# Products of zeros ahead of the first load: fp32r of several widths and divisions of the array in place of bf16 ones between the sums, with six more VectorE operations

## The chip, the cores and the metric

The kernel runs on one core of one Trainium2 chip. The metric is the device time of one execution in microseconds (us); runs of one kernel are compared by their median.

## The reference

Two layers of a diffusion trunk, over 256 latent and 256 context tokens of 2048 channels, all in float32. For each layer:

```
shift, scale, gate = split(silu(c) @ w_mod[l] + b_mod[l])        # the same with c_ctx for the context
h    = rmsnorm(x, g_pre[l]) * (1 + scale) + shift
proj = h @ w_in[l]                                               # 2048 x 5120 columns, nine groups
y    = concat(gated position mixing, windowed attention, Fourier mixing), each times its silu gate
x    = x + gate * rmsnorm(y @ w_out[l], g_post[l])
```

The context runs through the same weights, gives keys and values to the latent attention, and is updated in the first layer only. The output is the latent stream.

## The kernel before

x and the context are held transposed: 128 channels on the partitions (16 such blocks, numbered k), 512 tokens in the free dimension (256 latent, 256 context). A product with a float32 weight is made of fp32r products: ScalarE rounds the weight to a high part (`whi`, L535), VectorE subtracts for the low part (`wlo`, L537), and TensorE multiplies high by high, low by high and high by low (`mm3`, L566). The weights come in pieces of 128 x 1024 through three `raw` buffers, four `whi` and four `wlo` buffers (`Stream`, L462).

**The head** (L1483 to L1556) is written out by hand for TensorE, VectorE, ScalarE and SP: they keep the order of the text. SP and ScalarE issue eight loads of x, 512 KB each (L1488). VectorE clears constants and small buffers. Then a loop of 16 steps squares two blocks of x a step, on ScalarE, or on VectorE in steps 3, 8 and 13 (`XSQ`, L407), and TensorE sums the squares over the channels with a weight of ones of 32 columns (L1510). Four blocks go to four groups of 32 columns of the array (`tile_position=(0, 32 * ...)`). The squares lie in `w2k`, a tag of seven buffers, one of which holds the first constants until after the loop. When all is summed, ScalarE copies the sums (L1515), TensorE, VectorE and GpSimd make 1/rms of them (L1527, L593) and spread it over partitions (L1539), TensorE makes the first block of shift and scale (`Mod`, L173, products at L202, loads at L188), and `make_h0` (L664) makes the first h. Then **layer 0** begins: for each block k the products of three groups of columns (`ps_av`, at L802; `ps_au`, at L802 and L567), and beside them the shift and scale of block k + 1 from its 2 MB of modulation weights.

In the head stand products of zeros: `warm(idle, n)` (L607) issues n bf16 products of 128 columns of weights by 512, from the cleared tile `wz` (its name in the trace is `join`) to a bank of PSUM that nobody reads. In the loop stand 6 before the first step and 3 before steps 4, 8 and 12 (L1506); 2, 1 and 3 more stand behind the loop (L1522, L1534, L1551).

A tile that is asked for again under its tag takes the buffers in turn, and the new writer waits until the last reader of the old contents is through.

Of the kernel before, what the change touches and what calls it, by code (L numbers as in the profile page):

```python
# [7 lines left out]
F32 = mybir.dt.float32  # L8
F32R = mybir.dt.float32r
BF16 = mybir.dt.bfloat16  # L10
AF = mybir.ActivationFunctionType
ALU = mybir.AluOpType

P = 128
# [52 lines left out]
def trunk_kernel(ctx: ExitStack, tc: tile.TileContext, xT, xhalf, cT, wss, wsl, wmod, win, wout0, wout1, const, vec, rows,  # L67
                 wmat, bs, sink, out):
    nc = tc.nc
    V, A, G, PE, DMA = nc.vector, nc.scalar, nc.gpsimd, nc.tensor, nc.sync  # L70
# [6 lines left out]
    def sb(shape, dt, tag, bufs=1):  # L77
        cnt[0] += 1
        return pool.tile(shape, dt, tag=tag, bufs=bufs, name=f"{tag}_{cnt[0]}")

    def w2k(shape, dt=F32):
        return sb(shape, dt, "w2k", W2K)

    def mm_ps(name="mm"):
        cnt[0] += 1
        return psum.tile([P, 512], F32, tag="mm", bufs=6, name=f"ps_{name}_{cnt[0]}")

    def ms_ps(name="ms"):
        cnt[0] += 1
        return psum.tile([P, 512], F32, tag="ms", bufs=2, name=f"ps_{name}_{cnt[0]}")  # L90
# [19 lines left out]
    zero8 = sb([P, 8], F32, "zero8")  # L110
# [30 lines left out]
    def cc(name):  # L141
        o, w = COFF[name]
        return cst[:, o - P:o - P + w]

    def vc(l, name):
        o, w = VOFF[name]
        return vecs[:, l, o:o + w]
# [304 lines left out]
    NHI, NLO, NRAW = 4, 4, 3  # L452
# [9 lines left out]
    class Stream:  # L462
# [95 lines left out]
        def next(self):  # L558
            self.fetch()
            pace()  # L560
            self.pos += 1
            return self.out[self.pos - 1]
# [30 lines left out]
    def rstd_cols(sums, n, dim):  # L593
        t = sb([P, 4], F32, "rs_a", 2)
        V.tensor_scalar(out=t[:, :n], in0=sums, scalar1=1.0 / dim, scalar2=EPS, op0=ALU.mult, op1=ALU.add)
        r = sb([P, 4], F32, "rs_b", 2)
        G.tensor_tensor(out=r[:, :n], in0=t[:, :n], in1=mhalf[:, :n], op=ALU.pow)  # L597
        return r
# [6 lines left out]
    wz = sb([P, T], BF16, "join", 2)  # L605

    def warm(ps, n):  # L607

        for _ in range(n):
            PE.matmul(ps, wz[:, 0:P], wz, start=True, stop=True)  # L610
# [49 lines left out]
    def scale_x(k, rb, s, n=1):  # L660
        x = xx[2 * (k // 4) + s][:, k % 4:k % 4 + n]
        V.tensor_tensor(out=x, in0=x, in1=rb[:, s * S:(s + 1) * S].unsqueeze(1).to_broadcast([P, n, S]), op=ALU.mult)

    def make_h0(k, between=(), rb=None):  # L664

        new_h(k)
        t = w2k([P, T])
        for a, b in ((0, P), (P, S), (S, T)) if k == 1 else ((0, S), (S, T)):
            s = a // S
            if s and rb is not None:  # L670
                scale_x(k, rb, 1)
            A.activation(hh[k][:, a:b], x_at(k, a, b), AF.Identity, scale=gs[0][:, k, s:s + 1],
                         bias=sh[0][:, k, s:s + 1])
        next(iter(between), None)
        for s in range(2):
            sl = slice(s * S, (s + 1) * S)
            V.tensor_scalar(out=t[:, sl], in0=x_at(k, sl.start, sl.stop), scalar1=gs[0][:, k, s:s + 1],
                            scalar2=sh[0][:, k, s:s + 1], op0=ALU.mult, op1=ALU.add)
        V.tensor_tensor(out=hl[k], in0=t, in1=hh[k].bitcast(F32), op=ALU.subtract)
# [592 lines left out]
    def out_proj():  # L1272
        acc = sb([P, T], F32, "acc")
        cross = sb([P, T], F32, "kt1")
        state["phase"] = "out0"
        groups = [OUT[i] // 4 for i in range(0, KT, 4)]
        for g in groups[:2]:
            load_x0(g)
        for i, j in enumerate(OUT[:KT - HELD]):
            ps = tunit(T)  # L1280
            o_evac(j, ps, new_yo(j), acc, [0, 1], i == 0, cross)
            if i in (4, 8):
                load_x0(groups[1 + i // 4])
        held = []
        W.stop = len(W.src) // 2
        state["phase"] = ""
        for j in OUT[KT - HELD:]:
            held.append([W.next(), W.next()])
            ps = hold_unit(held[-1], LAT)
            o_evac(j, ps, new_yo(j), acc, [0], False, cross)  # L1290
        later.add(boundary(acc, cross), YX[0])
        W.stop = 0
        for _ in range(EARLY):
            W.emit()
        for i, j in enumerate(OUT[KT - HELD:]):
            ps = hold_unit(held[i], CTX)
            if i < HELD - 1:
                with low(200):
                    o_evac(j, ps, yo[j], acc, [1], False)
        state["late"] = lambda: o_evac(j, ps, yo[j], acc, [1], False)  # L1300
        later.flush()
        return acc
# [177 lines left out]

    EN = mybir.EngineType
    first_stage = ExitStack()
    with tc.manual_schedule(engines={EN.PE}):  # L1483

        first_stage.enter_context(tc.manual_schedule(engines={EN.DVE, EN.Activation, EN.SP}))
        G.dma_start(ct, cT)
        for i in range(8):
            (A if i == 1 else DMA).dma_start(xx[2 * (i % 4) + i // 4], xhalf[i // 4, i % 4])  # L1488
        raw = w2k([P, NFIRST])
        DMA.dma_start(raw, const[:, 0:NFIRST])  # L1490
        DMA.dma_start(vecs, vec)
        V.memset(wz, 0.0)
        A.activation(sb([P, 4], F32, "es", 2), zero4, AF.Silu)
        sq, idle = mm_ps("rs2"), mm_ps("idle")
        for i in range(KT):
            h, j = i // 8, i % 8
            x = xx[2 * (j // 2) + h][:, j % 2 * 2:j % 2 * 2 + 2]
            q = w2k([P, 2, S])
            if i in XSQ:
                V.tensor_tensor(out=q, in0=x, in1=x, op=ALU.mult)  # L1500
            else:
                A.activation(q, x, AF.Square)
            if i == KT // 2:
                A.activation(cs, ct, AF.Silu)
                V.tensor_copy(cpad[:, 2:].rearrange("p (k c) -> p k c", c=32)[:, :, 0:2], cs)
            if i % 4 == 0:  # L1506
                warm(idle, 3 if i else 6)
            for a in range(2):
                k = 2 * j + a
                PE.matmul(sq[32 * (k % 4):32 * (k % 4) + 32, h * S:(h + 1) * S], ones[:, 0:32], q[:, a],  # L1510
                          start=k < 4, stop=k >= KT - 4, tile_position=(0, 32 * (k % 4)))
        A.copy(identr, raw[:, 0:P])
        A.copy(cst[:, 0:NFIRST - P], raw[:, P:])
        row = w2k([P, T])
        A.copy(row, sq)  # L1515
        m = Mod(0)
        m.load()
        G.tensor_scalar(out=b1, in0=vc(0, "bmod")[:, 16:32], scalar1=1.0, scalar2=None, op0=ALU.add)
        G.tensor_tensor(out=b1g, in0=b1, in1=vc(0, "gpre"), op=ALU.mult)
        W.load()  # L1520
        m.rounds(1)
        warm(idle, 2)  # L1522
        r0 = []
        for h, ps in enumerate((ms_ps("rs"), mm_ps("rs"))):
            for j in range(2):
                c = slice(h * S + j * P, h * S + (j + 1) * P)
                PE.matmul(ps[:, j:j + 1], row[:, c], cc("sel")[:, 0:1], start=True, stop=True)  # L1527
            r0.append(rstd_cols(ps[:, 0:2], 2, D))
            if h == 0:
                sums = ps  # L1530
        ps = sums
        V.tensor_scalar(out=msx, in0=ps[:, 0:2], scalar1=1.0 / D, scalar2=EPS, op0=ALU.mult, op1=ALU.add)
        m.rounds(2)
        warm(idle, 1)  # L1534
        rb = ms_ps("rb")

        def spread(s):
            for j in (2 * s, 2 * s + 1):
                PE.matmul(rb[:, j * P:(j + 1) * P], r0[s][:, j % 2:j % 2 + 1].to_broadcast([P, P]), ident,  # L1539
                          start=True, stop=True)  # L1540

        spread(0)
        m.rounds(1)
        m.turn()
        scale_x(0, rb, 0)
        m.cols()
        spread(1)
        rb0 = sb([P, T], F32, "acc")
        e = W.emitting(512)
        next(e)  # L1550
        warm(idle, 3)  # L1551
        make_h0(0, e, rb)
        A.copy(rb0, rb)
        for s in range(2):
            scale_x(1, rb0, s, 2)
        state["e0"] = e  # L1556
        layer(0)
        state["acc"] = out_proj()
        layer(1)
        finish()  # L1560
# [77 lines left out]
```

## Time and profile before

| | us |
|---|---|
| median of 2 runs (1119.59 to 1120.44) | 1120.01 |
| span of the profiled execution, first to last instruction | 1117.0 |
| TensorE busy | 1107.8 (99%) |
| VectorE busy | 926.9 (83%) |
| ScalarE busy | 550.6 (49%) |
| GpSimd busy | 33.4 (3%) |
| first product of layer 0 (start, in the span) | 21.88 |

The profiled execution's own time is not listed beside its span; the median of the runs is 3.0 us above the span, and is used in its place.

How to read the lines: in the timeline each has its start, its length, the engine (PE is TensorE, PEld its loads of weights, DVE VectorE, ACT ScalarE, POOL GpSimd, SP the queue that issues loads), the line of the kernel, the operation, what it writes and reads, its shape, and how many were merged; in brackets stands how long the engine was idle before it, and what released it. A matmul's length holds the way through the array: products that follow each other start closer together than they are long, so their cost is read from start to start. In the groups of instructions the number behind the bar is the busy time of all, then the mean of one in ns. In the stretches (windows) the columns are length, busy time of TensorE, of its weight loads, VectorE, ScalarE and GpSimd, then the granted TensorE clock, the busy share of the DMA engines and GB/s. In the view of waits: who waited for what, us in total, how often, the longest.

### The profile page before, as it was taken

How to read it: one execution, taken by the hardware profiler on the slowest of the kernel's cores; microseconds unless marked ns; L12 is line 12 of the kernel's file. 1: busy time of each engine (PE TensorE's matmuls, PEld its weight loads, DVE VectorE, ACT ScalarE, POOL GpSimd, SP SyncE). 2: the span in 40 equal slices, each digit the busy share in tenths (PEclk: the TensorE clock that was granted, in tenths of full speed). 3: DMA queues.
4: the chain of work that ended last, by engine and by line, in shares of the span. 5: the costliest groups of instructions: out<-in, count | busy, mean ns of one | idle time of the engine just before them, and what ended most of it. 6: DMA issues, size and time to landing. Idle time of an engine off the chain costs nothing. (4 is left out here: it accounts for less than half of the span.)

```text
span 1117.0 us, 17368 instructions
## 1 busy us (share of the span) xinstructions
PE 1107.8 (99%) x6453; PEld 927.4 (83%) x6453; DVE 926.9 (83%) x1616; ACT 550.6 (49%) x1049; POOL 33.4 (3%) x43
## 2 busy tenths in 40 slices
PE   8999999999999999999999999999999999999998
PEld 4777888888888888888888888988888888888886
DVE  3677599999988897988999989496988789878883
ACT  4454823322235666632532324256665379867551
POOL 1000000000000000000000000030500000000000
PEclk9999999999999999999999999999999999999999
DMA  9999665567655343455466665385956686456972
GB/s 375 412 411 404 231 202 166 195 210 227 201 188 176 100 156 117 152 194 189 155 206 203 208 209 185 96 216 190 227 170 203 212 285 196 160 182 196 302 263 75
DMA packets 75525, 235.89 MB, mean 211 GB/s; under 512 B 8480, under 2 KB 15024, under 8 KB 75440
## 3 DMA queue, kind: packets, MB, share of 16 engines
q1 hardware_dynamic: 71088, 230.31, 61.4%
q0 software_dynamic: 4064, 3.69, 2.2%
q8 instruction: 50, 0.82, 0.3%
q10 hardware_dynamic: 288, 0.79, 0.2%
q14 instruction: 35, 0.29, 0.1%
HBM read 232.65 MB, written 2.10 MB: 210 GB/s over the span
## 5 line engine op out<-in xcount | busy, mean ns | idle before, releaser
L535 ACT CAST whi<-raw 128x1024 fp32r<-128x1024 f32 (+1 forms) x210 | 216.3, 1033 | 309.8 <-PE ps_t L568 203.0
L567 PE MATMUL ps_t<-hh,whi 128*128 128x512 f32 (+1 forms) x752 | 290.6, 386 | 0.0
L568 PE MATMUL ps_t<-hl,whi 128*128 128x512 f32 (+1 forms) x752 | 289.5, 385 | 0.0
L569 PE MATMUL ps_t<-hh,wlo 128*128 128x512 f32 (+1 forms) x752 | 289.5, 385 | 0.0
L537 DVE TENSOR_TENSOR wlo<-raw,whi 128x1024 fp32r<-128x1024 f32 (+1 forms) x210 | 251.2, 1200 | 42.3 <-ACT whi L535 36.0
L310 DVE SCALAR_TENSOR_TENSOR macc<-mraw,cs,macc 128x512 f32<-128x512 f32 x360 | 251.4, 746 | 13.8 <-DMA mraw<-in_wmod_dram 13.7
L723 PE MATMUL ps_t<-hh,whi 128*128 128x512 f32 x512 | 184.4, 398 | 0.0
L569 PEld LDWEIGHTS ps_t<-hh,wlo 128*128 128x128 f32 x752 | 141.3, 188 | 28.6
L567 PEld LDWEIGHTS ps_t<-hh,whi 128*128 128x128 f32 x752 | 141.3, 188 | 26.7
L568 PEld LDWEIGHTS ps_t<-hl,whi 128*128 128x128 f32 x752 | 141.4, 188 | 26.3
L724 PE MATMUL ps_t<-hh,wlo 128*128 128x256 f32 x512 | 143.4, 280 | 0.0
L723 PEld LDWEIGHTS ps_t<-hh,whi 128*128 128x128 f32 x512 | 96.1, 188 | 21.0
L724 PEld LDWEIGHTS ps_t<-hh,wlo 128*128 128x128 f32 x512 | 96.7, 189 | 0.4
L567 PE MATMUL ps_y<-whi,hh 128*128 128x512 f32 x104 | 41.4, 398 | 0.0
L569 PE MATMUL ps_y<-whi,hh 128*128 128x512 f32 x104 | 40.7, 391 | 0.0
L568 PE MATMUL ps_y<-wlo,hh 128*128 128x512 f32 x104 | 40.5, 390 | 0.0
L584 ACT CAST w2k<-ps_tp 128x512 fp32r<-128x512 f32 x40 | 23.4, 585 | 21.2 <-PE ps_scc L568 13.6
L585 DVE TENSOR_TENSOR w2k<-ps_tp,w2k 128x512 fp32r<-128x512 f32 x40 | 27.4, 686 | 3.5 <-ACT w2k L584 2.3
L597 POOL TENSOR_TENSOR rs_b<-rs_a,mhalf 128x2 f32<-128x2 f32 (+1 forms) x7 | 6.3, 897 | 751.8 <-DVE mx L1413 582.8
L1147 ACT ACTIVATE w2k<-w2k,den 128x512 f32<-128x512 f32 (+1 forms) x48 | 28.2, 647 | 0.7 <-DVE den L1142 0.6
L802 PE MATMUL ps_av<-whi,hh 128*128 128x512 f32 x64 | 24.4, 396 | 0.1
L567 PE MATMUL ps_o<-w2k,vv 128*128 128x256 f32 x80 | 24.4, 305 | 0.0
(493 smaller groups left out, 1822.6 us busy)
## 6 DMA issues: line engine op xcount, KB each, us to landing
raw<-in_win_dram SPq DMA_DIRECT2D x158, 512.0 KB, 4.2
mraw<-in_wmod_dram SPq DMA_DIRECT2D x128, 512.0 KB, 4.5
raw<-in_wout_dram SPq DMA_DIRECT2D x60, 512.0 KB, 4.5
mraw<-in_wsl_dram SPq DMA_DIRECT2D x12, 512.0 KB, 7.3
yy<-in_xhalf_dram SPq DMA_DIRECT2D x7, 512.0 KB, 7.4
mg<-in_wsl_dram SPq DMA_DIRECT2D x7, 512.0 KB, 8.7
mgl<-in_wsl_dram SPq DMA_DIRECT2D x7, 512.0 KB, 9.2
yy<-in_xhalf_dram POOLq DMA_DIRECT2D x28, 128.0 KB, 7.5
```

The lines of the kernel that those rows point to most:

```text
L310: V.scalar_tensor_tensor(out=acc[:, s], in0=w[:, kk % 2], scalar=c, in1=acc[:, s], op0=ALU.mult, op1=ALU.add)
L535: A.copy(ph, rc)
L537: self.last = V.tensor_tensor(out=pl, in0=rc, in1=ph.bitcast(F32), op=ALU.subtract)
L567: PE.matmul(ps, st[0], mv[0], start=start, stop=False)
L568: PE.matmul(ps, st[0], mv[1], start=False, stop=False)
L569: PE.matmul(ps, st[1], mv[0], start=False, stop=stop)
L584: A.copy(hi, src)
L585: V.tensor_tensor(out=lo, in0=src, in1=hi.bitcast(F32), op=ALU.subtract)
L723: PE.matmul(ps, w[0], h, start=k == 0, stop=False)
L724: PE.matmul(ps[:, 0:S], w[1], h[:, 0:S], start=False, stop=k == KT - 1)
L802: PE.matmul(ps, st[a], mv[b], start=start and (a, b) == (0, 0), stop=stop and (a, b) == (1, 0))
L1147: A.activation(prob[i][:, b * w:(b + 1) * w], prob[i][:, b * w:(b + 1) * w], AF.Copy, scale=den[:, c:c + 1])
```

## The change

`trial` is called once, after the bank `idle` is allocated and before the loop; `warm` goes from the loop. The three `warm` calls behind the loop stay.

```diff
+    def trial(idle):
+        z = sb([P, 1024], F32R, "whi", NHI)
+        o = sb([P, 1024], F32, "wlo", NLO)
+        V.memset(z.bitcast(F32), 0.0)
+        V.memset(o, 0.0)
+        banks = [idle] + [mm_ps("idle2") for _ in range(3)]
+        big = z[:, 0:512]
+        def go(n, kind):
+            for i in range(n):
+                if kind == "whole":
+                    PE.matmul(idle, z[:, 0:P], big, start=True, stop=True)
+                elif kind[0] == "rows":
+                    w = kind[1]
+                    h = w * (i % (P // w))
+                    PE.matmul(banks[i % (P // w)], z[h:h + w, 0:P], z[h:h + w, 0:512], start=True, stop=True,
+                              tile_position=(h, 0))
+                elif kind[0] == "narrow":
+                    PE.matmul(idle[0:kind[1]], z[:, 0:kind[1]], big, start=True, stop=True)
+                elif kind[0] == "short":
+                    PE.matmul(idle[:, 0:kind[1]], z[:, 0:P], z[:, 0:kind[1]], start=True, stop=True)
+                elif kind[0] == "bf":
+                    PE.matmul(idle[0:kind[1]], wz[:, 0:kind[1]], wz, start=True, stop=True)
+        go(6, ("bf", P))
+        go(3, ("short", P))
+        go(3, ("short", 256))
+        go(3, ("short", 384))
+        go(5, "whole")
+        go(8, ("rows", 64))
+        go(8, ("rows", 32))
+        go(3, ("narrow", 96))
+        go(3, ("bf", 96))
+        r = sb([P, 1024], F32, "raw", NRAW)
+        V.memset(r, 1.0)
+        for n in (512, 1024):
+            V.scalar_tensor_tensor(out=o[:, 0:n], in0=r[:, 0:n], scalar=zero8[:, 0:1], in1=o[:, 0:n], op0=ALU.mult, op1=ALU.add)
+            V.tensor_scalar(out=o[:, 0:n], in0=r[:, 0:n], scalar1=zero8[:, 0:1], scalar2=None, op0=ALU.mult)
+            V.tensor_tensor(out=o[:, 0:n], in0=r[:, 0:n], in1=o[:, 0:n], op=ALU.subtract)
...
         sq, idle = mm_ps("rs2"), mm_ps("idle")
+        trial(idle)
         for i in range(KT):
...
-            if i % 4 == 0:
-                warm(idle, 3 if i else 6)
             for a in range(2):
```

The trial takes one buffer each of `whi`, `wlo` and `raw` and three banks of PSUM. The pieces of weights that follow take the next buffers in turn; the third load of raw (L508) now takes the buffer that VectorE's six operations read.

TensorE's order in the loop, before, from the last of the first six products of zeros (`ps_idle`) to the second group of them; `ps_rs` are the sums, `w2k` the squares of steps 0 to 4, two blocks a row:

```order
L610 MATMUL ps_idle_112<-join_91 128x512
L1510 MATMUL ps_rs_27_111<-w2k_113,ones_72 32x256 x2
L1510 MATMUL ps_rs_27_111<-w2k_123,ones_72 32x256 x2
L1510 MATMUL ps_rs_27_111<-w2k_127,ones_72 32x256 x2
L1510 MATMUL ps_rs_27_111<-w2k_131,ones_72 32x256 x2
L610 LDWEIGHTS join_91
L610 MATMUL ps_idle_112<-join_91 128x512
```

The same place now: the last of the six bf16 products, then what stands between it and the sums (of the 16 products over 64 and 32 rows the first and the last two; `ps_idle_31` to `ps_idle_33` are the added banks), and the first sums:

```order
L1508 MATMUL ps_idle_112<-join_91 128x512
L1506 MATMUL ps_idle_112<-whi_113 128x128 x3
L1506 MATMUL ps_idle_112<-whi_113 128x256 x3
L1506 MATMUL ps_idle_112<-whi_113 128x384 x3
L1497 MATMUL ps_idle_112<-whi_113 128x512 x5
L1501 MATMUL ps_idle_112<-whi_113 128x512
...
L1501 MATMUL ps_idle_32_118<-whi_113 128x512
L1501 MATMUL ps_idle_33_119<-whi_113 128x512
L1504 MATMUL ps_idle_112<-whi_113 96x512 x3
...
L1552 MATMUL ps_rs_27_111<-w2k_170,ones_72 32x256 x2
L1552 MATMUL ps_rs_27_111<-w2k_174,ones_72 32x256 x2
```

All products of zeros of the loop stand ahead of the first sum now, 42 where 15 stood, and the 16 pairs of sums follow each other with nothing between them.

VectorE's order around its first square (`w2k`, from x in `yy`), before:

```order
L1492 MEMSET join_91 128x256
L120 MEMSET red_81 128x1 x2
L1500 TENSOR_TENSOR w2k_131<-yy_3_63 128x512
L1500 TENSOR_TENSOR w2k_154<-yy_2_62 128x512
L1505 COPY kt_16_79<-cs_78 128x16x2
```

And now:

```order
L120 MEMSET red_81 128x1 x2
L1488 MEMSET whi_113 128x1024
L1489 MEMSET wlo_114 128x1024
L1520 MEMSET raw_162 128x1024
L1522 SCALAR_TENSOR_TENSOR wlo_114<-raw_162,zero_14_76,wlo_114 128x512
L1523 TENSOR_SCALAR wlo_114<-raw_162,zero_14_76 128x512
L1524 TENSOR_TENSOR wlo_114<-raw_162,wlo_114 128x512
L1522 SCALAR_TENSOR_TENSOR wlo_114<-raw_162,zero_14_76,wlo_114 128x1024
L1523 TENSOR_SCALAR wlo_114<-raw_162,zero_14_76 128x1024
L1524 TENSOR_TENSOR wlo_114<-raw_162,wlo_114 128x1024
L1544 TENSOR_TENSOR w2k_182<-yy_3_63 128x512
```

The first square on VectorE, that of step 3, stands behind nine more operations; each of the last five of them reads or overwrites what the one before it wrote. ScalarE's and SP's orders are unchanged.

## The prediction

> **What bounds the kernel now.** The page first: its span and the share of TensorE; then the stretches of time (windows), to see whether the first stage is paced by TensorE or by the loads.
>
> ```profile
> span 1117.0 us, 17368 instructions
> PE 1107.8 (99%) x6453; PEld 927.4 (83%) x6453; DVE 926.9 (83%) x1616; ACT 550.6 (49%) x1049; POOL 33.4 (3%) x43
> 22.00:50.00 28.00, 27.97 (x339) 20.96 (x340) 16.61 (x38) 11.34 (x23) 0.00 (x0) 1.00 1.03 413
> 80.00:110.00 30.00, 30.00 (x365) 23.70 (x366) 23.59 (x46) 14.63 (x29) 0.00 (x0) 1.00 1.04 407
> ```
>
> TensorE is busy 99% of the span, and from 22 us on its busy column equals the length of the stretch. The DMA column (1.03, 1.04) is full there too, so both run level. Which of them sets the pace is read from the waits of the first 120 us:
>
> ```profile
> PEld ps_mod L202 <- DMA mraw<-in_wsl_dram: 0.3, 1, 0.3
> SPq L188 <- DMA mraw<-in_wsl_dram: 9.6, 12, 1.0
> ACT whi L535 <- DMA raw<-in_win_dram: 15.8, 5, 4.7
> ```
>
> TensorE waits for a load once, for 0.3 us; ScalarE's 15.8 us for raw weights are waits ahead of need (SP's row, from its own queue's waits, is for later). So TensorE is the pace, and what starts it later ends the kernel later. Where it starts is decided in the first 22 us, the only stretch that the change touches. The timeline:
>
> ```profile
> 2.03 2.74 PE L610 MATMUL ps_idle<-join 128*128 128x512 bf16 x6 [2.03 <-DVE red L120]
> 3.28 0.15 PEld L610 LDWEIGHTS <-join 128*128 128x128 bf16 x1 [0.28 <-issue]
> 3.71 0.15 PEld L610 LDWEIGHTS <-join 128*128 128x128 bf16 x1 [0.28 <-issue]
> 5.42 2.72 ACT L1502 ACTIVATE w2k<-yy 128x512 f32<-128x512 f32 x5 [2.76 <-DMA yy<-in_xhalf_dram]
> 5.63 0.69 DVE L1500 TENSOR_TENSOR w2k<-yy 128x512 f32<-128x512 f32 x1 [3.64 <-DMA yy<-in_xhalf_dram]
> 6.10 1.68 PE L1510 MATMUL ps_rs<-w2k,ones 128*32 128x256 f32 x16 [1.33 <-ACT w2k L1502]
> 7.71 0.82 PE L610 MATMUL ps_idle<-join 128*128 128x512 bf16 x3
> 9.41 0.21 ACT L1504 ACTIVATE cs<-ct 128x32 f32<-128x32 f32 x1
> 13.54 1.15 ACT L1502 ACTIVATE w2k<-yy 128x512 f32<-128x512 f32 x2 [0.73 <-DMA yy<-in_xhalf_dram]
> 14.22 1.15 PE L1510 MATMUL ps_rs<-w2k,ones 128*32 128x256 f32 x8 [0.17 <-ACT w2k L1502]
> 15.47 0.59 ACT L1515 COPY w2k<-ps_rs 128x512 f32<-128x512 f32 x1 [0.47 <-PE ps_rs L1510]
> 20.71 0.62 ACT L535 CAST whi<-raw 128x512 fp32r<-128x512 f32 x1 [4.65 <-DMA raw<-in_win_dram]
> 21.88 0.30 PEld L802 LDWEIGHTS ps_av<-whi,hh 128*128 128x128 f32 x2 [0.56 <-ACT hh L672]
> ```
>
> The sums of squares (L1510) follow the landing of x: the last two squares begin at 13.54, after a wait for x, end at 14.69, and the last sum ends at 14.22 + 1.15 = 15.37. From there a chain (copy, rstd, its spreading, the first modulation, hh) leads to the first product of layer 0 at 21.88. The fifteen products of zeros at L610 in this loop lie in TensorE's waits.
>
> **The change part by part.** Removed: those 15 bf16 products. They give back nothing by themselves, since the sums wait for x, whose last part lands at about 13.5 us. Added ahead of the sums in TensorE's order: 42 products; ahead of the square of step 3 in VectorE's: three memsets and six operations. The question is when TensorE is through with the 42 (call it T0), since no sum can start before.
>
> *Speed of TensorE.* The six bf16 products start 3.71 - 3.28 = 0.43 us apart; the three at 7.71 take 0.82 with a tail, about 0.22 each. The clock doubled in between. The view of the cores says when:
>
> ```profile
> core 0: 1117.0 us, clock 0.999
> ```
>
> A mean of 0.999 (0.9985 to 0.9995) is 0.6 to 1.7 us lost, so 1.1 to 3.4 us at half speed; counted from 2.03, with 3.71 still slow, it ended between 3.7 and 5.4. I take 4.9. fp32r at full speed, from later stretches:
>
> ```profile
> 700.20 0.39 PE L569 MATMUL ps_t<-hh,wlo 128*128 128x512 f32 x1
> 702.92 0.39 PE L569 MATMUL ps_t<-hh,wlo 128*128 128x512 f32 x1
> 163.02 0.28 PE L568 MATMUL ps_f<-mg,w2k 128*128 128x256 f32 x1
> 163.14 0.28 PE L569 MATMUL ps_f<-mg,w2k 128*128 128x256 f32 x1
> 162.80 0.19 PEld L567 LDWEIGHTS ps_f<-mg,w2k 128*128 128x128 f32 x1
> 162.91 0.19 PEld L568 LDWEIGHTS ps_f<-mg,w2k 128*128 128x128 f32 x1
> 46.56 1.08 PE L202 MATMUL ps_mod<-mraw,kt 128*32 128x128 f32 x32
> L202 PE MATMUL ps_mod<-mraw,kt 128*32 128x128 f32 x192 | 6.7, 276 | 0.0
> 46.56 0.81 PEld L202 LDWEIGHTS ps_mod<-mraw,kt 128*32 128x32 f32 x32 [0.35 <-issue]
> 48.45 0.30 PEld L802 LDWEIGHTS ps_av<-whi,hl 128*128 128x128 f32 x2 [0.20 <-issue]
> ```
>
> Twelve products of 512 columns from 700.20 to 702.92: 0.227 each. 256 columns: 0.12. Weights follow each other at 0.11, so 128 columns cost 0.11 (at half speed twice that), and 384, between 256 and 512, 0.17. The 32 products over column groups show that tiles side by side overlap: (1.08 - 0.28) / 32 = 0.03 each, where one alone would pass at 0.11. To and from such a division of the array the load of weights stands 0.35 and 0.20 us, about 0.2 of it unhidden.
>
> T0 with tiles overlapping: six bf16 end at 2.03 + 6 x 0.425 = 4.58; 3 of 128, the first two slow, 0.45, to 5.03; 3 of 256, 0.36, to 5.39; 3 of 384, 0.53, to 5.92; 5 of 512, 1.14, to 7.06; eight over 64 rows as four pairs, 0.2 + 0.92, to 8.18; eight over 32 rows as two fours, 0.2 + 0.46, to 8.84; three of 96 columns, 0.2 + 0.68, to 9.72; three bf16 of 96, 0.66, to 10.38; back to column groups 0.1: **T0 = 10.5**. No trace shows row groups. The two bounds are full overlap (10.5) and none, 4 + 6 more turns of 0.227, **12.8**. I take overlap, since the column groups, the nearest row, do overlap. If the clock doubles at 3.7, T0 falls by 0.5, at 5.4 it rises by 0.3. The Trainium skill ("TensorE: Matmul & The Clock Gate", Part 3 on packing) gives four row tiles of 512 columns 3.07 times the rate of one; by that the eight over 32 rows would take 0.6, as here with the switch; of two tiles it gives no figure, and no run here shows it.
>
> *VectorE.* The rows:
>
> ```profile
> 0.82 0.17 DVE L106 MEMSET ones<- 128x128 f32 x1 [0.82 <-PEq L1626]
> 1.07 0.49 DVE L116 MEMSET kt<- 128x514 f32 x1
> 1.92 0.07 DVE L120 MEMSET red<- 128x1 f32 x2
> L310 DVE SCALAR_TENSOR_TENSOR macc<-mraw,cs,macc 128x512 f32<-128x512 f32 x360 | 251.4, 746 | 13.8 <-DMA mraw<-in_wmod_dram 13.7
> L308 DVE TENSOR_SCALAR macc<-mraw,cs 128x512 f32<-128x512 f32 x24 | 10.7, 482 | 2.7 <-DMA mraw<-in_wmod_dram 2.6
> 25.90 0.33 SPq L508 DMA_DIRECT2D raw<-in_win_dram  x1
> L662 DVE TENSOR_TENSOR yy<-yy,acc 128x1024 f32<-128x1024 f32 x6 | 7.1, 1217 | 0.0
> ```
>
> Memset grows by (0.49 - 0.17) / 386 = 0.83 ns an element: 0.92 for 1024, three of them from 1.99 to 4.75; z is there at 2.9, before TensorE wants it at 4.6. Then 0.75 + 0.48 + 0.69 for 512 elements and, for 1024, 1.28 (bounds 0.75 and twice that), 0.75 (0.48 to 0.96), 1.22, with 0.05 for each dependence: 10.2. The square of step 3 (0.69, as at 5.63) ends at 10.9 in place of 6.3. TensorE needs it as the fourth sum, at about T0 + 0.5 = 11.0: it just hides behind T0; were TensorE free earlier, this would be the bound. The load of raw that now waits for VectorE is issued at 25.9, long after.
>
> *After T0.* The squares live in w2k, seven buffers, of which the constants hold one. So steps 0 to 5 are squared before T0, and step 6 waits until the first sum has freed its buffer: T0 + 0.7 (a square's end to its sum's end is 15.37 - 14.69 = 0.68 in the trace). From there ScalarE has eight squares at (2.72 - 0.61) / 4 = 0.53 apart and SiLU of c, 0.22: the last begins 7 x 0.53 + 0.22 = 3.93 later and lasts 0.61; its sum ends 0.68 after. In all T0 + 0.7 + 3.93 + 0.61 + 0.68 = T0 + 5.92, against 15.37: **delay = T0 - 9.45**. With 10.5 it is 1.05 us; with 12.8, 3.3 us. The lower end is 0: before T0 = 9.45 the landing of x decides as now.
>
> *What follows.* ScalarE's copy at 15.47, and by it the chain to 21.88, move by the delay. The weights (cast at 20.71) land when they did and are no longer close. After 22 us TensorE has no wait for a load to give the delay back from. The sum: 1117.0 + 1.05 = 1118.05 of span. The runs' median lies 3.0 above the profiled span (no time of the profiled execution itself is listed), so **1121.0 us**.
>
> **The rivals.**
>
> (a) *Row tiles do not overlap.* For it: no product over 64 or 32 rows stands in the trace, and weights of fp32 are loaded with each product. Against: column groups do overlap. 1120.0 + 3.3 = **1123.3**.
>
> (b) *Loads set the pace: not slower.* In 22 to 110 us the DMA is as full as TensorE. If the steps there really went at the loads' pace, a start 1 us later would only let the loads run ahead, and the end would stay. Place: the modulation weights at L202. It decides wherever their landing, not the end of the product before, releases TensorE. For it: 413 GB/s throughout, and SP waits for landings of earlier loads before it issues the next (9.6 us in the one row shown). Against: that single wait of 0.3 us. The whole 1.05 would be won back: **1120.0**.
>
> (c) *The clock falls back.* Between T0 and the first product of layer 0 TensorE now has only sums over 32 columns and short chain work, where three warm groups (7.71 and two later) stood before. If this counts as idle, TensorE runs at half speed from about 15 us until the dense work has filled some microseconds. Price from rows: 22 to about 25.4 at half speed loses 1.7, the chain's products from 15 to 22 about 1 more; with the delay of 1.05, 1120.0 + 3.75 = **1123.8**. For it: the three groups are gone. Against: by the rows at 6.10 and 14.22 TensorE is busy through most of the time of the sums themselves. The Trainium skill ("TensorE: Matmul & The Clock Gate", Part 1) has the clock halved after an idle window of 3.4 us; by that rule (c) needs the sums to count as idle, which no row here shows.
>
> **How the numbers follow.** Forecast 0.5, (a) 0.2, (b) 0.15, (c) 0.12; 0.03 for what I have not thought of. Time 1121.0. The range goes down to 1119.7, which holds (b) with half of the 0.9 us between the two runs, and up to 1123.8, which holds (a) and half of (c). All the cases lie within 4 us, 0.4%, while 2% (22.4 us), about what a measurement of this kernel can tell from no change, is far off: same 0.97, slower 0.02, faster 0.01.
>
> **What would show it.** In the profile after: six bf16 products 0.43 apart from 2.03; five of 512 columns 0.23 apart; the pairs over 64 rows starting together, and the fours; the first sum between 10 and 11, step 3's square from VectorE ending at about 10.9; the last sum ending near 16.4, ScalarE's copy at 16.5, the first product ps_av at 22.9; from there the same rows 1 us later to the end. Tiles at 0.23 us each mean (a); an unchanged time of the last ps_mod products near 117 us despite a later start means (b); products of ps_av 0.43 apart after 22 us mean (c). A first sum at 14 us or later, or a first stage that lengthens by more than the delay, would make the prediction wrong.

## The result and the profile after

The changed kernel takes 1133.95 us (median of 2 runs, 1133.09 to 1134.82) against 1120.01 us before: a ratio of 1.0124, with a 95% interval of 1.0095 to 1.0154. That is 13.9 us more, within 2%, slower by much more than the runs scatter, and above the forecast's range. The profiled execution took 1134.82 us; its page begins:

```profile
span 1133.0 us, 17429 instructions
PE 1124.0 (99%) x6477; PEld 934.6 (82%) x6480; DVE 935.8 (83%) x1625; ACT 550.8 (49%) x1049; POOL 33.8 (3%) x43
```

The span grew by 16.0 us (1133.0 against 1117.0), and TensorE's busy time by 16.2. (A run's time lies 1.8 us above its span: 1134.82 against 1133.0. So the profiled execution before took about 1118.8 us, less than either of the two runs behind the median of 1120.01, which is why the spans differ by more than the medians.) TensorE got no new wait to speak of: it is busy longer. The first question is how much of that lies in the head, where the change is. The timeline of the changed kernel, in the order of the prediction's steps (start, length, engine, line):

```profile
3.71 0.15 PEld L1508 LDWEIGHTS <-join 128*128 128x128 bf16 x1 [0.28 <-issue]
4.21 2.80 PE L1506 MATMUL ps_idle<-whi 128*128 128x128 f32 x9
6.81 1.42 PE L1497 MATMUL ps_idle<-whi 128*128 128x512 f32 x5
8.16 1.86 PE L1501 MATMUL ps_idle<-whi 64*128 64x512 f32 x16
9.95 0.94 PE L1504 MATMUL ps_idle<-whi 128*96 128x512 f32 x3
10.54 0.68 DVE L1544 TENSOR_TENSOR w2k<-yy 128x512 f32<-128x512 f32 x1
11.46 5.58 PE L1552 MATMUL ps_rs<-w2k,ones 128*32 128x256 f32 x62
16.87 0.39 PE L1552 MATMUL ps_rs<-w2k,ones 128*32 128x256 f32 x2
17.36 0.58 ACT L1557 COPY w2k<-ps_rs 128x512 f32<-128x512 f32 x1 [0.47 <-PE ps_rs L1552]
23.56 0.30 PEld L802 LDWEIGHTS ps_av<-whi,hh 128*128 128x128 f32 x2 [0.42 <-ACT hh L672]
```

The first sum starts at 11.46, and the first product of layer 0 at 23.56 in place of 21.88: 1.68 us later. So the head explains 1.7 of 16 us. Where do the rest arise? The groups of instructions give the first and the last start of each group (behind the three durations in ns), and the same group can be looked up in both kernels. Before:

```profile
L1029 PE MATMUL ps_mix<-ws,w2k x48: 270/275/348, 142.7 to 786.9; 128*128 128x128 f32 x48
L1225 PE MATMUL ps_v<-whi,hh x48: 389/398/403, 308.6 to 892.8; 128*128 128x512 f32 x48
L723 PE MATMUL ps_au<-hh,whi x32: 387/392/398, 730.4 to 762.0; 128*128 128x512 f32 x32
L1317 PE MATMUL ps_x<-identr,yy x32: 270/272/273, 1020.1 to 1053.4; 128*128 128x128 f32 x32
```

And after:

```profile
L1029 PE MATMUL ps_mix<-ws,w2k x48: 270/275/347, 145.6 to 800.3; 128*128 128x128 f32 x48
L1225 PE MATMUL ps_v<-whi,hh x48: 387/396/398, 314.7 to 907.1; 128*128 128x512 f32 x48
L723 PE MATMUL ps_au<-hh,whi x32: 392/394/396, 743.6 to 775.4; 128*128 128x512 f32 x32
L1317 PE MATMUL ps_x<-identr,yy x32: 270/272/273, 1034.8 to 1068.5; 128*128 128x128 f32 x32
```

The lag is 2.9 us at 142.7, 6.1 at 308.6, 13.2 at 730.4, 14.7 at 1020.1, and 16.0 at the end. It grows steadily through layer 0, hundreds of microseconds behind the last changed instruction, and only by another 2.8 us in layer 1. The stretches of time say what a growing lag without waits is. Before (length, then busy time and count of TensorE, of its weight loads, VectorE, ScalarE and GpSimd, then clock, DMA share and GB/s):

```profile
160.00:710.00 550.00, 550.00 (x2678) 461.89 (x2677) 495.15 (x801) 226.31 (x420) 0.00 (x0) 1.00 0.56 180
520.00:660.00 140.00, 140.00 (x620) 115.95 (x619) 128.88 (x188) 50.58 (x81) 0.00 (x0) 1.00 0.61 198
800.00:840.00 40.00, 40.00 (x241) 35.30 (x240) 36.34 (x76) 28.21 (x59) 1.75 (x1) 1.00 0.62 191
```

And after (the first and the last stretch moved by the lag):

```profile
163.00:723.00 560.00, 560.00 (x2677) 463.04 (x2676) 496.31 (x801) 226.42 (x419) 0.00 (x0) 1.00 0.56 177
520.00:660.00 140.00, 140.00 (x604) 113.58 (x603) 130.99 (x190) 49.32 (x77) 0.00 (x0) 1.00 0.61 196
814.00:854.00 40.00, 40.00 (x243) 35.65 (x243) 36.25 (x77) 28.58 (x62) 1.75 (x1) 1.00 0.62 185
```

The same 2677 products take 560 us where they took 550, at the same granted clock (1.00), with TensorE busy without a gap in both. Each product is slower: in 140 us of the products of 512 columns (L567 to L569), 604 pass where 620 did. By their start times they follow each other at 226.7 ns before and at 232.4 after (means over 520 to 660 us). In layer 1's stretch of alternating widths (800 to 840) nothing is lost. **One number carries the case: 5.7 ns per product, for products that the change doesn't touch.** The row of 520 to 660 us is the test in what follows, called the pace row: x620 is the old pace, x604 the slow one.

### The profile page after: what moved, and what is told of

It is laid out like the page before. It is cut to its first block, busy times and chain, and to the rows that moved or that the text cites. A ratio compares the mean times of both kernels' runs of the same rounds, so it can differ in the third digit from the quotient of the medians.

```text
span 1133.0 us, 17429 instructions
## 1 busy us (share of the span) xinstructions
PE 1124.0 (99%) x6477; PEld 934.6 (82%) x6480; DVE 935.8 (83%) x1625; ACT 550.8 (49%) x1049; POOL 33.8 (3%) x43
## 5 line engine op out<-in xcount | busy, mean ns | idle before, releaser
L567 PE MATMUL ps_t<-hh,whi 128*128 128x512 f32 (+1 forms) x752 | 294.0, 391 | 0.0
L569 PE MATMUL ps_t<-hh,wlo 128*128 128x512 f32 (+1 forms) x752 | 293.1, 390 | 0.0
L568 PE MATMUL ps_t<-hl,whi 128*128 128x512 f32 (+1 forms) x752 | 293.1, 390 | 0.0
L310 DVE SCALAR_TENSOR_TENSOR macc<-mraw,cs,macc 128x512 f32<-128x512 f32 x360 | 251.0, 743 | 11.5 <-DMA mraw<-in_wmod_dram 11.2
L569 PEld LDWEIGHTS ps_t<-hh,wlo 128*128 128x128 f32 x752 | 141.6, 188 | 31.7
L567 PEld LDWEIGHTS ps_t<-hh,whi 128*128 128x128 f32 x752 | 141.7, 188 | 29.6
L567 PE MATMUL ps_y<-whi,hh 128*128 128x512 f32 x104 | 41.7, 401 | 0.0
L569 PE MATMUL ps_y<-whi,hh 128*128 128x512 f32 x104 | 41.1, 395 | 0.0
L567 PE MATMUL ps_o<-w2k,vv 128*128 128x256 f32 x80 | 24.6, 307 | 0.0
```

The costliest lines, as they stand in the source:

```text
L310: V.scalar_tensor_tensor(out=acc[:, s], in0=w[:, kk % 2], scalar=c, in1=acc[:, s], op0=ALU.mult, op1=ALU.add)
L567: PE.matmul(ps, st[0], mv[0], start=start, stop=False)
L568: PE.matmul(ps, st[0], mv[1], start=False, stop=False)
L569: PE.matmul(ps, st[1], mv[0], start=False, stop=stop)
```

## The experiments

**Is it the chip, or the state in which TensorE's stream starts?** What could outlive the head? A way of streaming in which TensorE settles early (when its clock doubles while products run, or by the added kinds of products), or something that stays in place, such as where the tiles lie. Four kernels ran beside the kernel before (1119.70 us). `again` is the changed kernel, unaltered.

> The changed kernel once more, unaltered. What is to be explained: from the first product of layer 0 on, products of 512 columns in fp32r start 232.4 ns apart where they started 226.7 apart before, to the end of the kernel; the clock doubled at 7.0 us, while TensorE was streaming products of zeros, and at 4.9 us before, while it was idle. Theory 1 (the pace is set at the moment at which the clock doubles, by whether TensorE is streaming then): about 1134 us in every run in which the doubling falls into the stream, which here is nearly always. Theory 2 (the kinds of products set the pace): 1134 us in every run. Theory 3 (chance at each start): runs at both 1121 and 1134 us.

It took 1133.12 us (1.0121, 1.0106 to 1.0136), with x604 in the pace row: not the chip. `gap` lets TensorE stand idle ahead of the fp32r products. It moves VectorE's filling of `raw` and the first of the six operations ahead of the clearing of `z`; nothing is added:

```diff
-        V.memset(z.bitcast(F32), 0.0)
         V.memset(o, 0.0)
+        r = sb([P, 1024], F32, "raw", NRAW)
+        V.memset(r, 1.0)
+        V.scalar_tensor_tensor(out=o[:, 0:512], in0=r[:, 0:512], scalar=zero8[:, 0:1], in1=o[:, 0:512], op0=ALU.mult, op1=ALU.add)
+        V.memset(z.bitcast(F32), 0.0)
...
-        r = sb([P, 1024], F32, "raw", NRAW)
-        V.memset(r, 1.0)
...
```

> The same 42 products and VectorE operations, but z is cleared only after the clearing of r and the first VectorE operation, so that TensorE is idle from about 4.6 to 6.9 us, and all products of z come after that. Theory 1 (streaming at the doubling sets the pace): where the clock doubles in that gap, 226.7 ns per product of 512 columns in layer 0 and about 1121.5 us; where it doubles in the stream behind it, 232 ns and 1135 us. Theory 2 (kinds of products: all are there): 232 ns and 1134 us whatever the moment. A variant of theory 2, that the first fp32r products at half speed do it: 226.7 ns if the clock has doubled before 6.9 us.

1136.26 us (1.0144, 1.0127 to 1.0161), x604: the head is later still, the pace is as slow. By the trace's record of the clock it doubled at 10.5 us, in the stream behind the idle time, so this run does not tell the theories apart. `twelve` is the kernel before with twice the bf16 products ahead of the first sum, so that the clock doubles within an unbroken stream:

```diff
-                warm(idle, 3 if i else 6)
+                warm(idle, 3 if i else 12)
```

> The kernel before, with twelve bf16 products of zeros ahead of the first sum in place of six, so that TensorE streams from 2.0 to about 6.5 us without a pause, and no product of a new kind. Theory 1: the clock doubles in the stream, 232 ns per product of 512 columns, about 1134 us. Theory 2: no new kind, 226.7 ns and 1120 us.

1119.47 us (1.0000, 0.9990 to 1.0009). The pace is the old one, so the state of the stream at the doubling isn't the cause. The pace row of `twelve`:

```profile
520.00:660.00 140.00, 140.00 (x620) 115.91 (x619) 131.19 (x191) 50.50 (x81) 0.00 (x0) 1.00 0.61 201
```

`dve_only` has the change's tiles and VectorE operations, the old `warm` in the loop, and none of the new products:

```diff
-        go(6, ("bf", P))
...
-        go(3, ("bf", 96))
...
+            if i % 4 == 0:
+                warm(idle, 3 if i else 6)
```

> The kernel before with the new tiles (whi, wlo, raw, three banks) and all of the new VectorE operations, but without the new products; the bf16 products stand between the sums as before. Theories 1 and 2: 226.7 ns per product of 512 columns; the square of step 3 comes at 11 us in place of 6.3, so about 0.5 to 1 us later, 1121 us. A rival, that the buffers and banks, which are taken in another turn, make each product slower: 232 ns and 1134 us.

1135.29 us (1.0138, 1.0122 to 1.0153), although not one of the added products runs. Its pace row:

```profile
520.00:660.00 140.00, 140.00 (x604) 113.49 (x603) 132.39 (x193) 49.35 (x77) 0.00 (x0) 1.00 0.61 197
```

So the kinds of products fall too. What `dve_only` shares with the change are VectorE's operations and three tiles, asked for earlier than before.

**Where the tiles lie.** A tag gets its place in memory when it is first asked for. The trial asks for `whi`, `wlo` and `raw` ahead of all others of the head, and so moves them. The addresses in the built programs (bytes in a partition):

| | before | after |
|---|---|---|
| `whi`, first buffer | 105600 (128 modulo 256) | 74752 (0) |
| `wlo`, first buffer | 121984 (128) | 91136 (0) |
| `hh0` (all `hh` and `hl` alike modulo 256) | 138368 (128) | 138368 (128) |
| `hh0` - `whi`, modulo 256 | 0 | 128 |

TensorE reads `whi` or `wlo` and `hh` or `hl` in every one of the slowed products, one as weights, the other as the moving operand. Either the place of `whi` itself matters (theory A), or its distance to `hh` (theory R). Four kernels beside the kernel before (1119.54 us) set them against each other; the first three add no instruction to it, only small tiles that are there anyway are asked for earlier. `pair_shift` moves both by 128 bytes:

```diff
+        for tag in ("mx", "nm"):
+            sb([P, 4], F32, tag, 2)
         G.dma_start(ct, cT)
```

> The kernel before, in which 128 bytes of late small tiles (mx, nm) get their place ahead of the first loads. So the weights whi and wlo and the h tiles all lie 128 bytes further on: whi and hh start at 256 modulo 512 instead of 128, and their distance is as before. No work is added. Theory A (the absolute address of the weights sets the pace of an fp32r product: 128 modulo 256 is fast, 0 is slow): 232 ns per product of 512 columns, 1134 us. Theory R (the distance of weights and moving operand sets it): 226.7 ns, 1120 us.

`h_shift128` puts the same 128 bytes between `wlo` and `hh0`, so that `whi` stays and only the distance becomes 128:

```diff
         rb0 = sb([P, T], F32, "acc")
         e = W.emitting(512)
         next(e)
+        for tag in ("mx", "nm"):
+            sb([P, 4], F32, tag, 2)
```

> The kernel before, in which the same 128 bytes get their place between wlo and hh0: the weights stay at 128 modulo 512, hh and hl move to 256, so that the distance is 128, as in the changed kernel. No work is added. Theory R: 232 ns per product of 512 columns, 1134 us. Theory A of the weights: 226.7 ns, 1120 us. Theory A of the moving operand (128 fast, 0 modulo 256 slow): 1134 us, but then the changed kernel, whose hh lie where they lay before, is not explained.

`h_shift256` puts 256 bytes there (`mx`, `nm`, `den`, `skb`, `nskb`).

> As the one before with 256 bytes between (mx, nm, den, skb, nskb): weights at 128 modulo 512, hh and hl at 384. Theory R modulo 256: fast, 1120 us. Theory R modulo 512 or more: slow, 1134 us. Theory A: fast, 1120 us, by the weights' address as by the moving operand's modulo 256.

`after_aligned` is the whole change, with 128 bytes ahead of `whi`, so that the distance is 0 again:

```diff
+        for tag in ("rs_a", "rs_b"):
+            sb([P, 4], F32, tag, 2)
         G.dma_start(ct, cT)
```

> The changed kernel with all of its work, in which 128 bytes of small tiles (rs_a, rs_b) get their place ahead of the first new tile: whi and wlo lie at 128 modulo 512, as in the kernel before, and hh stay at 128, so the distance is 0 modulo 512 again. Theories A and R: 226.7 ns per product of 512 columns; what is left is the later start, 1.7 us: about 1121.7 us. If the new order of the tiles does it in another way (distances of several KB, the turn of buffers or banks): 232 ns and 1134 us.

The pace rows of `pair_shift`, `h_shift128`, `h_shift256` and `after_aligned`:

```profile
520.00:660.00 140.00, 140.00 (x619) 115.93 (x618) 129.92 (x189) 51.01 (x82) 0.00 (x0) 1.00 0.62 199
```

```profile
520.00:660.00 140.00, 140.00 (x604) 113.53 (x603) 129.41 (x188) 49.90 (x78) 0.00 (x0) 1.00 0.62 195
```

```profile
520.00:660.00 140.00, 140.00 (x620) 115.95 (x619) 128.96 (x188) 50.88 (x82) 0.00 (x0) 1.00 0.61 198
```

```profile
520.00:660.00 140.00, 140.00 (x619) 115.96 (x618) 131.38 (x192) 51.85 (x82) 0.00 (x0) 1.00 0.62 202
```

`pair_shift` took 1118.67 us (0.9995, 0.9986 to 1.0004): theory A falls. `h_shift128`, with no work added at all, took 1131.87 (1.0112, 1.0095 to 1.0129): 12.3 us for 128 bytes. `h_shift256` took 1119.36 (0.9997, 0.9988 to 1.0006): it is the distance modulo 256. `after_aligned` took 1120.56 (1.0012, 1.0003 to 1.0021): with the distance mended, the change's own work costs 1.0 us (0.3 to 2.4). It keeps the changed turn of the buffers and the three added banks, so these are not the cause.

**How the pace goes with the distance.** Four more kernels, beside the kernel before (1119.64 us), put other sizes at the same place as `h_shift128`: `skb` (32 bytes), `skb` and `nskb` (64), or `mx`, `nm` and `den` (192).

> The kernel before with 32 bytes (skb) between wlo and hh0, so that hh minus whi is 32 modulo 256. What is asked is how finely the distance counts. If 256 bytes are eight banks of 32 and a conflict arises only half a turn away: 226.7 ns per product of 512 columns, 1119.5 us. If any distance other than 0 modulo 256 costs: 232 ns, 1132 us. If the cost rises with the distance up to 128: about 228 ns, 1123 us.

> The same with 64 bytes (skb, nskb): distance 64 modulo 256. Half a turn only: 226.7 ns, 1119.5 us. Anything but 0: 232 ns, 1132 us. Rising with the distance: about 229.5 ns, 1126 us. A pace better than 226.7 ns is possible too; that would be a kernel faster than both.

> The same with 192 bytes (mx, nm, den): distance 192 modulo 256. It shows whether the cost is the same at 64 on either side of 128: the same time as with 64 bytes, if only the distance modulo 256 counts and its sign does not.

`hi_apart` asks for `whi` first and puts the 128 bytes behind it, so that `hh` lies 128 from `whi` but 0 from `wlo`. It asks whether only the products over `whi` suffer:

```diff
         rb0 = sb([P, T], F32, "acc")
+        sb([P, 1024], F32R, "whi", NHI)
+        for tag in ("mx", "nm"):
+            sb([P, 4], F32, tag, 2)
```

> The kernel before with 128 bytes (mx, nm) between whi and wlo, so that hh minus whi is 128 modulo 256 and hh minus wlo is 0. Of the three products of a piece two read whi and one wlo. If each product pays by its own two operands: products that read whi about 232 ns, that with wlo 226.7, on the mean 230.5, and about two thirds of the loss, 1128 us. If what counts is how the loading of one product's weights lies to the operand of the product that runs meanwhile: it is the same two thirds, but shifted by one in the order (the product ahead of the one whose weights are read pays). If any unequal distance unsettles all: 232 ns for all three, 1132 us.

| kernel | `hh` - `whi`, `hh` - `wlo` modulo 256 | pace row | us | ratio and interval |
|---|---|---|---|---|
| h_shift32 | 32, 32 | x602 | 1132.14 | 1.0113 (1.0098 to 1.0128) |
| h_shift64 | 64, 64 | x613 | 1125.68 | 1.0053 (1.0038 to 1.0067) |
| h_shift192 | 192, 192 | x601 | 1133.51 | 1.0123 (1.0108 to 1.0138) |
| hi_apart | 128, 0 | x601 | 1132.23 | 1.0112 (1.0095 to 1.0129) |

At 64 about half is lost (6.0 us), at 192 all of it, so the sign matters. In `hi_apart` the third of the products whose distance is 0 gains nothing: by the start times all three lines are at 232 to 235 ns. A product is thus not slowed by its own pair alone.

**Whose reads are they?** VectorE and ScalarE write `whi`, `wlo` and `hh` while TensorE reads them. `curve` has the addresses of `after_aligned`, with this in place of the trial's products, its six VectorE operations and its filling of `raw`:

```diff
+        go(30, ("bf", P))
+        for base in (0, 32):
+            for d in (0, 16, 32, 64, 96, 128, 160, 192, 224):
+                s = base + P + d // 4
+                for _ in range(32):
+                    PE.matmul(idle, z[:, base:base + P], z[:, s:s + 512], start=True, stop=True)
```

> In place of the trial stand 30 bf16 products and 18 groups of 32 fp32r products of zeros, 128 columns of weights by 512; no VectorE operation is added. In a group the weights and the moving operand lie in one tile, with the moving operand's address 0, 16, 32, 64, 96, 128, 160, 192 or 224 bytes (modulo 256) behind that of the weights; the nine groups are made twice, the second time with both addresses 128 bytes further on. The rest of the kernel lies as in after_aligned. Theory R1 (TensorE's own reads of weights and of the moving operand disturb each other when their addresses differ modulo 256): groups at 0 start 227 ns apart, those at 32, 64, 128, 192 bytes 229 to 235, alike for both bases. Theory R2 (the distance matters only while VectorE and ScalarE use the same tiles): all 18 groups at 227 ns, since no other engine uses the tile. Rest of the kernel at 226.7 ns by both; the whole about 1120 + 18 x 32 x 0.227 - 10 = 1241 us, as the sums wait for the products.

The stretches of `curve`, each from the start of a group to the start of the next. In order: distance 0 (its last 22 products, second base), 16 (first and second base), 64 (first, second), 128 (first, second), 160 (first, second). The counts hold one product or load that began earlier:

```profile
80.01:85.00 4.99, 4.99 (x23) 4.13 (x22) 0.00 (x0) 0.00 (x0) 0.00 (x0) 1.00 0.01 3
18.14:25.55 7.41, 7.41 (x33) 6.01 (x32) 0.00 (x0) 0.00 (x0) 0.00 (x0) 1.00 1.04 394
85.00:92.41 7.41, 7.41 (x33) 6.01 (x32) 0.00 (x0) 0.00 (x0) 0.00 (x0) 1.00 0.00 0
33.02:40.34 7.32, 7.32 (x33) 6.01 (x32) 0.00 (x0) 0.00 (x0) 0.00 (x0) 1.00 0.00 0
99.88:107.20 7.32, 7.32 (x33) 6.01 (x32) 0.00 (x0) 0.00 (x0) 0.00 (x0) 1.00 0.00 0
47.81:55.28 7.47, 7.47 (x33) 6.01 (x32) 0.00 (x0) 0.00 (x0) 0.00 (x0) 1.00 0.01 2
114.68:122.14 7.46, 7.46 (x33) 6.01 (x32) 0.00 (x0) 0.00 (x0) 0.00 (x0) 1.00 0.00 0
55.28:62.77 7.49, 7.49 (x33) 6.02 (x32) 0.00 (x0) 0.00 (x0) 0.00 (x0) 1.00 0.00 0
122.14:129.64 7.50, 7.50 (x33) 6.02 (x32) 0.00 (x0) 0.00 (x0) 0.00 (x0) 1.00 0.00 0
```

Per product: 4.99 / 22 = 0.2268 us at distance 0; 7.41 / 32 = 0.2316 at 16; 0.2288 at 64; 0.233 at 128; 0.234 at 160 (32, 96, 192 and 224 lie at 0.233 to 0.234 too). Both bases give the same to 0.01 us in 7.4. VectorE, ScalarE and GpSimd did nothing (0.00), and the pace at 16 is the same with 394 GB/s of loads and with none. So TensorE's own two reads are enough: theory R1 holds, R2 falls. The whole kernel took 1253.8 us in its one run, against 1119.17 before on that chip, where 1241 was expected. The sums wait for all these products, and the first of them starts at 144.66: by the prediction's T0 - 9.45 that makes 135.2 us more, and 134.6 were measured.

The Trainium skill ("TensorE: Matmul & The Clock Gate", Part 2, on LDWEIGHTS) says that loading the next tile's weights doesn't steal read bandwidth from the running matmul, since TensorE has two independent read ports. The rows don't agree fully: with nothing but an address changed, the same products and weight loads take up to 3% longer.

**Is there more to gain?** The kernel before is itself slower than 227 ns in some stretches (229 to 230 by the start times in 360 to 480 us), where products over `w2k`, `vv` and `mraw`, which lie elsewhere modulo 256, stand between the big groups. `all_aligned` is the kernel before with its small tiles asked for in an order that puts every operand of these products at 128 modulo 256:

```diff
-    identr = sb([P, P], F32R, "identr")
...
+    sb([P, 4], F32, "rs_a", 2)
+    sb([P, 8], F32, "skb")
+    identr = sb([P, P], F32R, "identr")
     cpad = sb([P, 2 + KT * 32], F32, "kt0")
...
+        sb([P, 4], F32, "es", 2)
+        sb([P, 8], F32, "nskb")
         G.dma_start(ct, cT)
...
         rb0 = sb([P, T], F32, "acc")
+        for tag in ("mx", "nm", "den"):
+            sb([P, 4], F32, tag, 2)
```

> The kernel before, with small buffers allocated in another order, so that all operands of products (w2k, mraw, macc, vv, kt, identr beside whi, wlo, hh, mg, yy) start 128 bytes behind a multiple of 256; no instruction is added or removed. In the kernel before whi, wlo, hh lie so already, and products over w2k (192), mraw, macc and vv (0), kt (32) don't. Theory R1 (the distance modulo 256 of TensorE's own two reads): products between those of L567 to L569 no longer disturb them; where the kernel before runs at 229 to 230 ns (22 to 220 and 320 to 490 us) it comes near 227, about 600 and 650 products by 1 to 2.5 ns, and some 100 products over w2k by 6 ns: 1 to 4 us faster, 1116 to 1119. If the disturbance there is the change of widths and not the addresses: 1119.5 as before. In 500 to 700 us 226.7 ns by both.

1120.80 us against 1119.59 (1.0010, 1.0001 to 1.0019): the 1 to 4 us that I expected by R1 did not come. It is 1.2 us slower instead, for a cause that stays open. The stretch of 320 to 490 us on TensorE alone, before:

```profile
320.00:490.00 170.00, 170.00 (x906) 1.00 0.47 147
```

and in `all_aligned`:

```profile
320.00:490.00 170.00, 170.00 (x905) 1.00 0.46 149
```

The same count: what keeps that stretch off 227 ns isn't these distances. That it is the change of widths there is argued, not shown. Layer 1 points the same way: where products of 512 and 256 columns take turns (800 to 840 us), a pair takes 355 ns by the start times at distance 0 (before) and 352 at 128 (after), so there the equal addresses gain nothing. No kernel of this study beats the kernel before by more than its interval.

## Why the prediction was wrong, point by point

- **TensorE is the pace, and a later start ends the kernel later**: right. Rival (b), loads that give the delay back, did not occur. `after_aligned` shows it best, since its pace is the old one: its first product of layer 0 is 2.1 us late (23.96 against 21.89), and its span still 1.8 (1118.8 against 1117.0).
- **T0 = 10.5**: measured 11.46. One term was mis-sized, the moment at which the clock doubles. The nine products of 128, 256 and 384 columns took 2.60 us (4.21 to 6.81) where I had 1.34: they ran at half speed to the end. The doubling came at 7.0, not 4.9. In `again` they took 1.93, and the first sum began earlier:

```profile
4.21 2.08 PE L1506 MATMUL ps_idle<-whi 128*128 128x128 f32 x9
6.14 1.32 PE L1497 MATMUL ps_idle<-whi 128*128 128x512 f32 x5
10.69 5.58 PE L1552 MATMUL ps_rs<-w2k,ones 128*32 128x256 f32 x62
```

  The upper bound for that moment (5.4) came from a misreading: the mean clock of 0.999 says nothing of the head. The stretches of the kernel before show where the 0.1% is lost (the clock is the third number from the right):

```profile
0.00:4.50 4.50, 2.47 (x6) 0.73 (x6) 1.11 (x8) 1.49 (x2) 0.94 (x5) 1.00 0.55 188
1114.00:1117.00 3.00, 0.00 (x0) 0.00 (x0) 0.00 (x0) 0.00 (x0) 0.00 (x0) 0.54 0.46 172
```

  In the first 4.5 us the column says 1.00, though the products there start 0.43 us apart: the trace's record of the clock begins only with the doubling. The loss, 0.46 x 3.00 = 1.4 us, lies at the end, when TensorE is through. By that record the doubling in this execution came at 4.91, so my 4.9 was right for it, but by luck; and the moment differs between executions. The Trainium skill ("TensorE: Matmul & The Clock Gate", Part 1) says so: the window that is watched runs on freely, whenever the kernel starts. That agrees with 7.0 and 5.3 for the same program, and should have widened T0 from the start.
- **Row tiles overlap**: right, and rival (a) falls. From the first of the 16 products over 64 and 32 rows to the first of 96 columns there are 9.95 - 8.16 = 1.79 us; the step gave 0.92 + 0.2 + 0.46 + 0.2 = 1.78.
- **VectorE just hides behind T0**: right. Its square of step 3 ran from 10.54 to 11.22, 0.3 us later than predicted. With T0 at 11.46 that is early enough; with my 10.5 the fourth sum, due at 11.0, would have waited for it.
- **The last sum at T0 + 5.92**: right within 0.12 us, and by the way foreseen: ScalarE's square of step 6 waited for the first sum and began at 12.19, T0 + 0.73. With the measured T0 that is 17.38; the last sum ended at 16.87 + 0.39 = 17.26, and ScalarE's copy, which waits for it, began at 17.36. The first product of layer 0 came 1.68 us later than before, where T0 - 9.45 gives 2.0. Rival (c), a clock that falls back, did not occur: 16 products of the first modulation (L202) between the sums and layer 0 take 0.65 us before (at 17.09) and after (at 18.98), and all stretches behind them show 1.00.
- **The price of the change's work, 1.05 us**: within what `after_aligned` shows, 1.0 us (0.3 to 2.4). That the two agree so closely is partly luck: T0 is 10.7 in `again`, 11.5 after and 11.9 in `after_aligned`, which by T0 - 9.45 makes 1.2 to 2.4.
- **"From there the same rows 1 us later to the end"**: this is the step that failed, and with it the forecast of 1121.0 and its range. The sum has no term for the pace of layer 0: it was taken as unchanged, without a reason, and no rival changes it for more than a few microseconds. I had the pieces of weights only "take the next buffers in turn", and never asked where the tiles lie. They moved `whi` and `wlo` to 128 modulo 256 from `hh`; products of 512 columns in layer 0 then followed the one before them 3 to 6 ns later (5.7 in the pace row). Over 160 to 710 us alone that is the 10 us between 550 and 560. Layer 1's stretch of 800 to 840 us, with 512 and 256 columns in turn, loses nothing (x241 and x243): the lag stands still there.

`h_shift128` and `after_aligned` are the two halves of the proof: the distance without the work costs 12.3 us, the work without the distance 1.0, and together they make 13.3 of the 13.9 measured (13.4 in `again`). Why equal addresses modulo 256 are the good case stays open; no run here looks inside the reads.

## What to carry to other kernels

An edit that asks for a tile earlier moves other tiles, and so can change the pace of products that it doesn't touch: compare the addresses of the operands, modulo 256, in both built programs before costing the edit at its own work (shown here for fp32r products of 512 columns in a row). When a lag grows steadily with no new wait, count the products of one kind in equal stretches; a count tells 5.7 ns a product apart, which no duration of a single row shows. A small edit that "should cost nothing" is separated from its side effects by two kernels: the side effect without the work, and the work with the side effect undone.

## What was not expected of the hardware

- Products of 128 columns of fp32r weights by 512 follow each other at 226.8 ns when weights and moving operand lie at equal addresses modulo 256, and at 228.8 to 234.2 ns at eight other distances; 64 bytes cost least (2.0 ns), 160 most (7.4). In `hi_apart` a third of the products at distance 0 didn't help.
- At distance 0 the good pace isn't there at once: in the second group of that distance in `curve`, the first ten products start 224 to 236 ns apart, and 226 or 227 from then on.
- The clock doubled at very different moments after the same start of work at 2.03: by the traces' records at 4.9 us in the kernel before, 7.0 after, 5.3 in `again`, 14.7 in `dve_only`. The kernel's work need not differ for that: `pair_shift` has the head of the kernel before, instruction by instruction, and there it doubled at 12.5. Its groups of three bf16 products (0.82 us at full clock) show it, and so do its first 16 sums (2.44 us, against 1.68 in the kernel before):

```profile
6.48 2.44 PE L1512 MATMUL ps_rs<-w2k,ones 128*32 128x256 f32 x16 [1.70 <-ACT w2k L1504]
8.85 1.46 PE L610 MATMUL ps_idle<-join 128*128 128x512 bf16 x3
...
12.11 0.99 PE L610 MATMUL ps_idle<-join 128*128 128x512 bf16 x3
...
14.03 0.82 PE L610 MATMUL ps_idle<-join 128*128 128x512 bf16 x3
```

- In all 16 traces the stretch at full clock lasts a whole multiple of 3.4133 us (1109.33 us, 325 of them, in the kernel before; 1122.99, 329, after), by the traces' records, as if it changed only at the borders of windows of that length.
